# Residual rows in three steps, stores issued by ScalarE, modulated rows split out of PSUM, and four modulation vectors moved to the end of the first MLP

## The chip, the cores and the metric

One core of a Trainium2 chip runs the whole program. The metric is the device time of one execution in microseconds (us); less is better. PE is TensorE (matmuls, transposes), DVE is VectorE, ACT is ScalarE, POOL is GpSimd, and SP is SyncE, which here only issues DMA transfers. Each engine executes its own instruction stream strictly in order and meets the others at semaphores.

## The reference

Two layers of a diffusion trunk, 640 tokens (128 of a context, 512 latent ones) of width 1024, all fp32. Both layers modulate their input by six vectors that come from a condition, and end each sub-layer in a post-norm:

```python
def _adaln(cond, w, b):                       # w: 1024 x 6144, one per layer
    m = jax.nn.silu(cond) @ w + b
    return jnp.split(m[:, None, :], 6, axis=-1)

def _modulate(x, shift, scale):
    return x * (1 + scale) + shift

def _residual_norm(x, y, gate, g, b):
    return _layernorm(ALPHA * x + gate * y, g, b)

def _ffn(h, w1, w2):
    return jnp.square(jax.nn.relu(h @ w1)) @ w2
```

Layer 0 mixes by grouped-query attention and, beside it, a depthwise convolution of width 31; layer 1 by a bidirectional mLSTM whose gates run through scans over time. Each mixer has an output projection, `_residual_norm`, an MLP of width 4096 and again `_residual_norm`.

## The kernel before

The 640 tokens are five tiles of 128 rows; `acc` holds them in SBUF and `acc_d` in DRAM. Every large product is made to fp32 accuracy from three matmuls: an operand x is split into a high part (`whi`, `act_h`, cast on ACT) and a low part (`wlo`, `act_l`, a subtraction on POOL or DVE), and L193 to L195 multiply high by high, high by low and low by high. A weight piece is therefore a DMA into `raw` (L149), a cast (L166) and a subtraction (L167).

The program runs in stages, read from the trace: start, first modulation and the combined input projection until 180 us, with the convolution's taps (L965 on DVE, L972 on POOL) running beside it from 63 us on; twelve attention units until about 325 us, the convolution's LayerNorm (`conv_norm`, first matmul L1255) towards their end; the attention's output projection until 385; the first MLP until about 812, and behind it its tail: the last product `down(7)`, and for each tile the LayerNorm, four transposes per half (L375), the modulation and the first value projection of the mLSTM (`put_v`, head 0); then head 1 and the gates' product until 925; the mLSTM until 1214; its output projection until 1285; the second MLP until the end at 1735.

What sets the order: the program is written once in the order of the mathematics, and a list scheduler with a timeline model orders each engine's stream from it, with priorities. An instruction that waits for a buffer or for data stops all that stands behind it on its engine. For SP this holds too: a store whose data isn't there holds up the loads behind it.

Modulation vectors (1024 columns each) are made in background work. `ada_steps` yields after each of eight steps; a step loads 512 KB of `w_ada` and runs four matmuls of 32 output partitions side by side (L293); after the eighth comes one DVE addition (L297), and either a store (`gate_d`, for the two gate vectors of a layer) or two transposes (L305) and four copies. `background(n)` runs the next n steps of the `pending` list where it is called. Three vectors are made beside the input projection; seven, (0,5) and (1,0) to (1,5), during attention, because `ADA_IN_ATT = 7`; the attention's units call `background(7)` each. Vector (0,5) is the gate of the first MLP, and (1,0) and (1,1) modulate the rows that leave its tail; (1,2) to (1,5) are not needed before the mLSTM's output projection, at 1214 us.

The MLP keeps `acc_d` as the place of the residual: during the loop over its middle units, `residual(t, j)` loads half a row tile into `rx` (one buffer), multiplies and adds the LayerNorm's gain and bias on POOL (L445), and stores it. At the MLP's end `finish_mid` does per tile the LayerNorm and `modulate_T`:

```python
for half in range(2):
    pt = ...                                       # PSUM, four transposes into it
    h = scr(t, half)                               # SBUF
    affine(pt, half * 4, h, A, B, c, ...)          # L357 on DVE, L361 on ACT: h <- pt * A + B
    nc.scalar.copy(out=act_h, in_=h)               # L381
    nc.vector.tensor_tensor(out=act_l, in0=h, in1=act_h, op=subtract)   # L382
```

The output projection adds the gated product in 256-wide pieces (`add_gated`, L451 and L452): the first half of the columns through `s` and POOL, the second half in PSUM on DVE. `finish_mixer` stores `acc` to `acc_d` from SP; so does `put_v` its `v_d` pieces (L1397), and the tail its rows (L1431).

Of the kernel before, what the change touches and what calls it, by code (L numbers as in the profile page):

```python
# [18 lines left out]
P = 128  # L19
# [48 lines left out]
GEMMS = "01k2qr3"  # L68
ADA_IN_ATT = 7
FAST = (1, 3)  # L70
FIRST_DVE = ()
FIRST_HI = ((0, 0, 0), (0, 0, 1), (0, 1, 0), (0, 1, 1))
WIDE = False
AFF_DVE = (4,)
# [18 lines left out]
def trunk_kernel(ctx: ExitStack, tc: tile.TileContext, I, O):  # L93
# [231 lines left out]
    def drain():  # L325
        while pending:
            background()
# [37 lines left out]
    def modulate_T(src, t, A, B, scr, halves=(0, 1), second=nc.vector):  # L365

        ah, al = act
        c = 0 if t == 0 else 1
        sl = slice(t * P, (t + 1) * P)
        pt2 = None if K.startup else ps2()  # L370
        for half in halves:
            pt = psP.tile([P, 512], F32, name="po") if K.startup and t % 2 else ps1() if K.startup else pt2[:, half, :]
            for q in range(4):
                k = half * 4 + q
                nc.tensor.transpose(out=pt[:, q * P:(q + 1) * P], in_=src[:, k * P:(k + 1) * P], identity=ident)  # L375
            h = scr(t, half).rearrange("p (q n) -> p q n", n=P)
# [58 lines left out]

    def load_ln(lt, l, s, scale):
        nc.sync.dma_start(out=lt[:, 0, :], in_=I["ln_g"][l, s:s + 1, :].broadcast_to([P, D]))
        nc.sync.dma_start(out=lt[:, 1, :], in_=I["ln_b"][l, s:s + 1, :].broadcast_to([P, D]))
        if scale != 1.0:
            nc.scalar.mul(out=lt, in_=lt, mul=scale)  # L440
# [112 lines left out]
    class Sub:  # L553
# [51 lines left out]
        def rows(self, scale):  # L605
            self.gate, self.lnt = self.two_rows(), self.aux.tile([P, 2, D], F32, name="lnt")
            load_gate(self.gate, self.l, 0)
            load_ln(self.lnt, self.l, 0, scale)

# [5 lines left out]

        def residual(self, t, j):

            d = acc_d[:, t, j * 512:(j + 1) * 512]
            x = self.aux.tile([P, 512], F32, name="rx")
            nc.sync.dma_start(out=x, in_=d)  # L620
            residual_from(x, self.lnt, j, nc.gpsimd)
            nc.sync.dma_start(out=d, in_=x)

# [5 lines left out]
        def finish_mixer(self, key):  # L629
# [26 lines left out]
            def fin(t):  # L656
# [16 lines left out]
                if hi > HT:  # L673
                    b = max(lo, HT)
                    put("B12", self.h32[0][:, :, b:hi], slice(b - HT, hi - HT), PUT[2])
                    put("B22", self.h32[1][:, :, b:hi], slice(b - HT, hi - HT), PUT[3])
                nc.sync.dma_start(out=acc_d[:, t, :], in_=acc[:, t, :])
                if t and not COMB_LATE:
# [5 lines left out]

    def ffn(l, S, finish, ln_scale, prepare=None, ahead=None):
        w1, w2 = I["w_ff1"][l], I["w_ff2"][l]
# [105 lines left out]
        for j in range(6):  # L792
            for i in range(2):
                u = 2 * j + 2 + i
                h[u] = hidden(up(u))
                background(3)
                down(j, (h[2 * j], h[2 * j + 1]), i)
                if j < NT:
                    S.residual(j, i)
                background(2)  # L800
# [11 lines left out]
        S.lnt = late.tile([P, 2, D], F32, name="lnt")  # L812
        scr = late.tile([P, 4, 512], F32, name="scr")
        S.scratch = lambda t, half: scr[:, (t % 2) * 2 + half]
        rs0 = load_resid(0)
# [3 lines left out]
        pieces = [down_weights(7, c) for c in range(2)]  # L819
        load_ln(S.lnt, l, 1, ln_scale)  # L820
        rs1 = load_resid(1)
# [501 lines left out]
    def finish_mid(key, S):  # L1323
        def fin(t):
            layernorm(t, t == NT - 1)
            modulate_T(acc[:, t, :], t, *AB[key], S.scratch, second=nc.vector if t >= LATE_DVE else nc.scalar)
        return fin

    def finish_last(S):
        def moments(t):  # L1330

            x = acc[:, t, :]
            nm = smallp.tile([P, 1], F32, name="fl_m")
            if t in ACT_STATS:
                var = smallp.tile([P, 1], F32, name="fl_v")
                s, q = (smallp.tile([P, 2], F32, name=f"fl_{y}") for y in "sq")
                for j in range(2):
                    nc.scalar.activation(
                        out=S.scratch(t, j), in_=x[:, j * 512:(j + 1) * 512], func=AF.Copy, accum_out=s[:, j:j + 1])
                nc.vector.tensor_scalar(  # L1340
                    out=nm, in0=s[:, 0:1], scalar1=s[:, 1:2], scalar2=-1.0 / D, op0=ALU.add, op1=ALU.mult)
                for j in range(2):
                    nc.scalar.activation(
                        out=S.scratch(t, j), in_=x[:, j * 512:(j + 1) * 512], func=AF.Square, bias=nm[:, 0:1],
                        accum_out=q[:, j:j + 1])
# [47 lines left out]
    def put_v(ws, h, t, ps, tmp):  # L1393

        tm_tile(ws, act, t, ps[:, 0:256])
        nc.scalar.copy(out=tmp[:, 0:256], in_=ps[:, 0:256])
        nc.sync.dma_start(out=v_d[:, h, t], in_=tmp[:, 0:256])  # L1397

    with Sub(0) as S:
        S.rows(ALPHA)  # L1400
        out_proj(I["w_out_a"][0], S, S.finish_mixer("f0"))
        K.ada_m = lambda: S.fp.tile([P, 256], F32, name="ada_m")
        pending += [ada_vec(*x) for x in ada_late[ADA_IN_ATT:]]
        v_w = []

        def v_ahead():
            psum_plan(2, PS_D7)
            if PS_D7 < 3:
                K.psV = K.psum.enter_context(tc.tile_pool(name="psV", bufs=1, space=PSUM, reuse_waits="tile"))
            else:  # L1410
                K.psV = psC
# [11 lines left out]
        ffn(0, S, finish_and_v, ALPHA, lambda: mod_cols(1, 0, lng(0, 1), lnb(0, 1), *AB["m1"]), v_ahead)  # L1423
# [19 lines left out]
    with ExitStack() as ms:  # L1443
# [303 lines left out]
        def state(h, keys):  # L1747

            for d, (kwh, kwl) in enumerate(keys):
                cs = m2.tile([P, DEC], F32, name="wt").rearrange("p (a b) -> p a b", a=2)  # L1750
                for j in range(2):
# [5 lines left out]
                    nc.vector.tensor_copy(out=ncol[:, c0:c0 + 1], in_=ps[:, 256:257])  # L1757
                nc.sync.dma_start(
                    out=O["new_state_c"][0, 0, d, h].rearrange("(k p) v -> p k v", p=P), in_=cs)
# [122 lines left out]
    with Sub(1) as S:  # L1882
        S.rows(ALPHA)
        out_proj(I["w_out_m"][0], S, S.finish_mixer("f1"))
        ffn(1, S, finish_last(S), 1.0)

# [41 lines left out]
```

## Time and profile before

| what | before |
|---|---|
| median of 3 runs (lowest to highest) | 1737.89 us (1736.95 to 1741.92) |
| the profiled execution's own time | 1737.0 us |
| its span in the trace | 1735.2 us |
| mean granted TensorE clock | 0.971 of full speed |
| busy: PE, DVE, POOL, ACT | 1607.3, 1098.1, 1005.4, 796.3 us |
| PE idle in the span | about 128 us |

The time outside the span, 1.8 us, is the program's launch and end. [...] A row of groups gives busy time, mean duration of one instruction in ns, and behind the second bar the engine's idle time just before them with what ended it. Where an engine is shown as waiting for another, the wait is that of an in-order stream: what stands behind it waits as well.

### The profile page before, as it was taken

Reading aid. Unit: us, or ns where it says so; the run is one execution under the profiler, and the core shown is the slowest. Engines: PE = TensorE matmul, PEld = TensorE weight load, DVE = VectorE, ACT = ScalarE, POOL = GpSimd, SP = SyncE. Lnnn points to the kernel's source line nnn. Section 1 sums busy time; section 2 is a strip of 40 time slices with the busy share of each in tenths; the row PEclk is TensorE's granted clock in tenths of the full one; section 3 lists DMA queues with packets and bytes.
Section 4 is the critical chain, followed back from the end, with each engine's and each line's share of the span. In section 5 each row is a group of like instructions: output and inputs, shape, how many; then the busy total and the mean of one; then the engine's idle time right before and its main releaser. Section 6 shows DMA issues by size and latency. Waiting matters only on the chain. (4 is left out here: it accounts for less than half of the span.)

```text
span 1735.2 us, 27401 instructions
## 1 busy us (share of the span) xinstructions
PE 1607.3 (93%) x10155; PEld 1412.7 (81%) x10155; DVE 1098.1 (63%) x1924; ACT 796.3 (46%) x1560; POOL 1005.4 (58%) x760
## 2 busy tenths in 40 slices
PE   7988899998989999999788998997989999999996
PEld 4678555898879989987678998897979889989885
DVE  2899997669434444356875687778498354344367
ACT  2224666345444344343543555556265444344343
POOL 2246474247955546548654766756459756546565
PEclk8999999998999999999999999999999999999998
DMA  9852885323432213216223222235442323213241
GB/s 307 256 185 75 268 306 178 71 101 119 130 85 92 92 56 97 86 61 206 83 69 103 71 84 91 98 98 194 123 152 85 125 89 98 89 57 98 85 158 61
DMA packets 151309, 211.76 MB, mean 122 GB/s; under 512 B 11845, under 2 KB 92969, under 8 KB 151176
## 3 DMA queue, kind: packets, MB, share of 16 engines
q1 hardware_dynamic: 150944, 209.94, 37.4%
q8 instruction: 80, 1.31, 0.3%
q14 instruction: 53, 0.43, 0.1%
q10 hardware_dynamic: 232, 0.08, 0.0%
HBM read 186.74 MB, written 23.24 MB: 121 GB/s over the span
## 5 line engine op out<-in xcount | busy, mean ns | idle before, releaser
L167 POOL TENSOR_TENSOR wlo<-raw,whi 128x512 fp32r<-128x512 f32 x374 | 518.6, 1410 | 412.2 <-ACT whi L166 397.5
L166 ACT CAST whi<-raw 128x512 fp32r<-128x512 f32 x368 | 224.7, 620 | 429.2 <-PE ps L195 192.1
L193 PE MATMUL ps<-whi,h 128*128 128x512 f32 x640 | 254.5, 399 | 11.0 <-DVE pr L526 5.7
L194 PE MATMUL ps<-wlo,h 128*128 128x512 f32 x640 | 254.6, 398 | 0.3 <-POOL wlo L167 0.3
L195 PE MATMUL ps<-whi,h 128*128 128x512 f32 x640 | 253.6, 396 | 0.0
L193 PE MATMUL ps<-act_h,whi 128*128 128x320 f32 (+2 forms) x704 | 221.2, 316 | 8.5 <-ACT act_h L625 7.5
L194 PE MATMUL ps<-act_l,whi 128*128 128x320 f32 (+2 forms) x704 | 221.3, 315 | 5.5 <-DVE act_l L626 3.1
L195 PE MATMUL ps<-act_h,wlo 128*128 128x320 f32 (+2 forms) x704 | 220.9, 314 | 2.2 <-POOL wlo L167 2.2
L167 POOL TENSOR_TENSOR wlo<-s,whi 128x512 fp32r<-128x512 f32 x118 | 163.9, 1393 | 67.2 <-ACT whi L166 61.9
L758 DVE TENSOR_TENSOR acc<-acc,ps 128x512 f32<-128x512 f32 x120 | 81.8, 685 | 162.0 <-PE ps L195 162.0
L193 PEld LDWEIGHTS ps<-whi,h 128*128 128x128 f32 x640 | 121.3, 190 | 40.2 <-DVE pr L526 6.0
L193 PEld LDWEIGHTS ps<-act_h,whi 128*128 128x128 f32 x704 | 135.3, 192 | 13.2 <-ACT act_h L625 7.9
L195 PEld LDWEIGHTS ps<-whi,h 128*128 128x128 f32 x640 | 121.3, 190 | 29.2
L194 PEld LDWEIGHTS ps<-wlo,h 128*128 128x128 f32 x640 | 121.5, 190 | 28.1 <-POOL wlo L167 1.2
L194 PEld LDWEIGHTS ps<-act_l,whi 128*128 128x128 f32 x704 | 134.9, 192 | 8.9 <-DVE act_l L626 3.9
L195 PEld LDWEIGHTS ps<-act_h,wlo 128*128 128x128 f32 x704 | 134.9, 192 | 3.1 <-POOL wlo L167 3.1
L193 PE MATMUL ps<-whi,act_h 128*128 128x256 f32 x440 | 126.1, 290 | 0.3 <-DVE acc L1095 0.3
L194 PE MATMUL ps<-wlo,act_h 128*128 128x256 f32 x440 | 124.7, 287 | 0.0
L195 PE MATMUL ps<-whi,act_l 128*128 128x256 f32 x440 | 123.8, 287 | 0.0
L972 POOL TENSOR_TENSOR cy<-cy,tap 128x655 f32<-128x655 f32 x50 | 80.3, 1606 | 54.0 <-DVE cy L965 22.6
L193 PE MATMUL ps<-T_h,whi 128*128 128x320 f32 x336 | 103.7, 309 | 1.6 <-ACT pr L550 1.6
L166 ACT CAST whi<-s 128x512 fp32r<-128x512 f32 x120 | 73.2, 616 | 67.3 <-DVE s L501 54.9
(437 smaller groups left out, 4066.0 us busy)
## 6 DMA issues: line engine op xcount, KB each, us to landing
raw<-in_w_ff_dram SPq DMA_DIRECT2D x128, 512.0 KB
whi<-in_w_ada_dram SPq DMA_DIRECT2D x80, 256.0 KB
wlo<-in_w_ada_dram SPq DMA_DIRECT2D x80, 256.0 KB
raw<-in_w_in_m_dram SPq DMA_DIRECT2D x32, 512.0 KB
ada_w<-in_w_ada_dram SPq DMA_DIRECT2D x32, 256.0 KB
acc_d<-acc SPq DMA_DIRECT2D x15, 512.0 KB
raw<-in_w_in_a_dram SPq DMA_DIRECT2D x12, 512.0 KB
rx<-acc_d SPq DMA_DIRECT2D x20, 256.0 KB
```

Source lines behind the costliest of these rows:

```text
L166: nc.scalar.copy(out=hv, in_=src)
L167: (eng or nc.gpsimd).tensor_tensor(out=lv, in0=src, in1=f32(hv), op=ALU.subtract)
L193: nc.tensor.matmul(out=out, lhsT=lh, rhs=rh, start=start, stop=False)
L194: nc.tensor.matmul(out=out, lhsT=lh, rhs=rl, start=False, stop=False)
L195: nc.tensor.matmul(out=out, lhsT=ll, rhs=rh, start=False, stop=stop)
L758: nc.vector.tensor_tensor(out=x, in0=x, in1=ps, op=ALU.add)
L972: nc.gpsimd.tensor_tensor(out=y, in0=y, in1=tp, op=ALU.add)
```

## The change

- `ADA_IN_ATT` is 3: attention makes (0,5), (1,0) and (1,1), with the calls of `background` scaled to 3 a unit. The other four vectors enter `pending` in `v_ahead`, that is with the last product of the first MLP. Their 32 steps run at `background(5)` behind each of the five tiles of the tail, `background(1)` behind each value projection that follows, and a `drain`. Their weights go through `adaw`, 512 KB a step, three buffers.
- `WIDE` is on: the second half of an output projection goes through one 512-wide PSUM tile and one pair of 512-wide additions on DVE for each tile of rows.
- `modulate_T` of the tail writes the modulated rows back into PSUM; cast and subtraction read them there. The `scr` tile is gone but for the last LayerNorm.
- `residual(step)` has three parts that belong to three pieces: store of piece n-2, POOL work on piece n-1, load of piece n. `rx` has three buffers, the gain and bias tile half its size, loaded and scaled twice.
- Stores of `acc` in `finish_mixer`, of `v_d` and of `new_state_c` are issued by ACT.
- `put_v` uses its own one-buffer PSUM pool in the tail and the two-buffer pool `ps1` behind it, since `psc` now serves the vectors.

```diff
-ADA_IN_ATT = 7
+ADA_IN_ATT = 3
-WIDE = False
+WIDE = True
...
-            h = scr(t, half).rearrange("p (q n) -> p q n", n=P)
+            h = (scr(t, half) if K.startup else pt).rearrange("p (q n) -> p q n", n=P)
...
-        def residual(self, t, j):
-            d = acc_d[:, t, j * 512:(j + 1) * 512]
-            x = self.aux.tile([P, 512], F32, name="rx")
-            nc.sync.dma_start(out=x, in_=d)
-            residual_from(x, self.lnt, j, nc.gpsimd)
-            nc.sync.dma_start(out=d, in_=x)
+        def residual(self, step):
+            def rows(n):
+                return acc_d[:, n % NT, (n // NT) * 512:(n // NT + 1) * 512]
+            n = step - 2
+            if 0 <= n < 2 * NT:
+                nc.sync.dma_start(out=rows(n), in_=self.rx.pop(n))
+            n = step - 1
+            if 0 <= n < 2 * NT:
+                if n % NT == 0:
+                    nc.scalar.mul(out=self.lnt, in_=self.lnt, mul=self.scale)
+                residual_from(self.rx[n], self.lnt, 0, nc.gpsimd)
+            n = step
+            if n < 2 * NT:
+                if n % NT == 0:
+                    self.lnt = self.aux.tile([P, 2, 512], F32, name="lnt")
+                    load_ln(self.lnt, self.l, 0, (n // NT) * 512)
+                self.rx[n] = self.aux.tile([P, 512], F32, name="rx", bufs=3)
+                nc.sync.dma_start(out=self.rx[n], in_=rows(n))
...
-                nc.sync.dma_start(out=acc_d[:, t, :], in_=acc[:, t, :])
+                nc.scalar.dma_start(out=acc_d[:, t, :], in_=acc[:, t, :])
...
-                if j < NT:
-                    S.residual(j, i)
+                S.residual(2 * j + i)
...
-        nc.sync.dma_start(out=v_d[:, h, t], in_=tmp[:, 0:256])
+        nc.scalar.dma_start(out=v_d[:, h, t], in_=tmp[:, 0:256])
...
-        pending += [ada_vec(*x) for x in ada_late[ADA_IN_ATT:]]
...
+            K.psV = K.psum.enter_context(tc.tile_pool(name="psV", bufs=1, space=PSUM, reuse_waits="tile"))
             hv = [S.h_tile() for _ in range(2)]
+            K.ada_raw = lambda: S.late_pool.tile([P, D], F32, name="adaw", bufs=3)
+            pending.extend(ada_vec(*x) for x in ada_late[ADA_IN_ATT:])
...
-                put_v(v_w[0], 0, t, psC.tile([P, 512], F32, name="psc"), S.pr())
+                put_v(v_w[0], 0, t, K.psV.tile([P, 512], F32, name="psv"), S.pr())
+            background(5)
...
-            put_v(v_w[h], h, t, (psC if h == 0 else K.psV).tile([P, 512], F32, name="psc"), S.pr())
+            put_v(v_w[h], h, t, ps1(), S.pr())
+            background(1)
+        drain()
+        nc.scalar.mul(out=S.lnt, in_=S.lnt, mul=ALPHA)
```

PE's stream in the attention's early units, before (`kTA`, `kTB`: scores; `pT`: weights times values; `psc<-whi` and `psc<-wlo`: the two halves of an `ada` step):

```order
L1226 MATMUL po<-pT,vS 64x256 x2
L1200 MATMUL ps_2621<-ident,pp 128x128 x2
L293 MATMUL psc<-wlo,stat 32x256
L293 MATMUL psc<-whi,stat 32x256 x2
L293 MATMUL psc<-wlo,stat 32x256 x2
L1187 MATMUL ps_2753<-kTA,qT 128x320
L1187 MATMUL ps_2753<-kTB,qT 128x320
```

The same part of PE's stream with the change (its scores are L1197 there):

```order
L1236 MATMUL po<-pT,vS 64x256 x2
L1215 MATMUL ps_2509<-pT,vS 64x128 x2
L1150 MATMUL ps_2539<-identr,qs 128x128 x4
L1197 MATMUL ps_2596<-kTA,qT 128x320
L1197 MATMUL ps_2596<-kTB,qT 128x320
```

Up to this place both streams hold the same `ada` matmuls; from here on before has those of four vectors between the scores, and the change none.

PE's stream in the tail of the first MLP, with the change (`ps<-whi,h`: `down(7)`; `ident,acc`: transposes of a finished tile; `psv`: value projection):

```order
L195 MATMUL ps_8436<-whi,h 128x512
L193 MATMUL ps_8568<-whi,h 128x512
L194 MATMUL ps_8568<-wlo,h 128x512
L195 MATMUL ps_8568<-whi,h 128x512
L293 MATMUL psc<-adaw,stat 32x256
L375 MATMUL ps_8193<-ident,acc 128x128 x4
L293 MATMUL psc<-adaw,stat 32x256 x3
L375 MATMUL ps_8327<-ident,acc 128x128 x4
L193 MATMUL ps_8568<-whi,h 128x512
```

The 128 new matmuls stand in 22 places between `down(7)`, the transposes and the value projections; the last 20 of them, five steps, stand in one piece ahead of the 46 matmuls that precede the gates' product.

SP's stream between the value projections and the gates, before (`gwr`: the gates' weights; `nm_d<-g_ab`: the gates' result on its way to `mb`):

```order
L1397 DMA v_d<-pr 128x256
L1431 DMA acc_d<-acc 128x1024 x2
L1503 DMA gwr<-in_w_in_m_dram 128x8x16
L1513 DMA gb<-in_b_gate_m_dram 4x1 x3
L1397 DMA v_d<-pr 128x256 x2
L1513 DMA gb<-in_b_gate_m_dram 4x1
L1520 DMA m0c<-in_state_m_dram 4x1 x2
L1397 DMA v_d<-pr 128x256 x5
L149 DMA raw<-v_d 128x1024
L1397 DMA v_d<-wt 128x256
L149 DMA raw<-v_d 128x256
```

SP's stream from the last stores of finished rows to the gates, with the change:

```order
L1448 DMA acc_d<-acc 128x1024
L290 DMA adaw<-in_w_ada_dram 128x1024
L277 DMA ada_m<-in_b_ada_dram 4x256 x2
L290 DMA adaw<-in_w_ada_dram 128x1024 x4
L149 DMA raw<-v_d 128x1024
L290 DMA adaw<-in_w_ada_dram 128x1024
L149 DMA raw<-v_d 128x256
L300 DMA gate_d_1_8973<-ada_m 128x256
L149 DMA raw<-in_w_in_m_dram 128x4x256 x2
L1520 DMA gwr<-in_w_in_m_dram 128x8x16
L1530 DMA gb<-in_b_gate_m_dram 4x1 x4
```

The stores of `v_d` have left SP, and the load of the gates' weights, which stood ahead of most of them, now stands behind the last `adaw` load and behind the store of the last vector, `gate_d_1`.

## Rows read from the trace of the kernel before

**Rows 1.** The page's first part: busy time, share of span, instructions.
```profile
PE 1607.3 (93%) x10155; PEld 1412.7 (81%) x10155; DVE 1098.1 (63%) x1924; ACT 796.3 (46%) x1560; POOL 1005.4 (58%) x760
```

**Rows 2.** Windows in the attention; stretch, length, busy by engine, clock, DMA share, GB/s.
```profile
180.00:200.00 20.00, 14.52 (x124) 7.42 (x116) 18.08 (x35) 11.04 (x27) 9.00 (x7) 0.83 0.79 261
200.00:220.00 20.00, 17.42 (x146) 9.82 (x144) 19.02 (x40) 14.16 (x32) 11.54 (x10) 1.00 0.87 290
...
180.00:290.00 110.00, 99.85 (x817) 53.32 (x810) 96.31 (x194) 72.59 (x155) 65.77 (x46) 0.97 0.81 278
290.00:330.00 40.00, 39.31 (x273) 29.11 (x272) 33.48 (x75) 19.68 (x39) 2.54 (x2) 0.96 0.17 47
```

**Rows 3.** The same windows for line L293 alone, PE: the modulation vectors' matmuls.
```profile
180.00:290.00 110.00, 43.53 (x436) 0.97 0.81 278
...
180.00:183.00 3.00, 2.42 (x38) 1.00 0.86 264
```

**Rows 4.** Lines L972 and L1255: count, duration min/median/max, first and last start.
```profile
L972 POOL TENSOR_TENSOR cy<-cy,tap x50: 1339/1582/2670, 131.2 to 270.0; 128x655 f32<-128x655 f32 x50
...
L1255 PE MATMUL psc<-cy,ones x24: 274/326/433, 289.3 to 296.9; 128*128 128x128 f32 x8, 128*128 128x192 f32 x8, 128*128 128x320 f32 x8
```

**Rows 5.** Windows around the first MLP's tail and the value projections.
```profile
780.00:812.00 32.00, 29.33 (x153) 25.77 (x152) 21.20 (x25) 15.65 (x24) 27.37 (x20) 0.96 0.65 216
812.00:871.00 59.00, 49.21 (x266) 41.91 (x264) 45.44 (x99) 26.40 (x56) 37.61 (x28) 0.93 0.29 95
871.00:925.00 54.00, 42.82 (x311) 41.27 (x311) 35.70 (x44) 23.98 (x44) 30.39 (x21) 0.94 0.28 86
```

**Rows 6.** What PE waited for, 812 to 925: total us, times, longest.
```profile
PE psc L195 <- DVE act_l L382: 6.2, 3, 3.4
PE psc L193 <- ACT pr L1396: 4.5, 4, 1.7
PE psi L193 <- ACT wt L1396: 4.5, 1, 4.5
```

**Rows 7.** DVE groups, 812 to 875: busy us, mean ns, idle before.
```profile
L382 DVE TENSOR_TENSOR act_l<-scr,act_h 128x512 fp32r<-128x512 f32 x10 | 10.0, 1003 | 0.0
L451 DVE TENSOR_TENSOR ps<-ps,gate 128x512 f32<-128x512 f32 x6 | 4.1, 684 | 0.3 <-PE ps L195 0.3
L452 DVE TENSOR_TENSOR acc<-acc,ps 128x512 f32<-128x512 f32 x6 | 4.1, 677 | 0.1
```

**Rows 8.** DVE groups in the first output projection, 355 to 410.
```profile
L451 DVE TENSOR_TENSOR ps<-ps,h 128x256 f32<-128x256 f32 x10 | 4.3, 427 | 8.4 <-PE ps L195 8.4
L452 DVE TENSOR_TENSOR acc<-acc,ps 128x256 f32<-128x256 f32 x10 | 4.2, 415 | 0.2
```

**Rows 9.** Windows at the two MLPs' starts.
```profile
375.00:400.00 25.00, 23.79 (x196) 22.79 (x194) 24.48 (x46) 16.63 (x42) 17.56 (x13) 1.00 0.46 153
400.00:425.00 25.00, 18.53 (x88) 17.82 (x88) 24.79 (x22) 11.36 (x19) 16.95 (x8) 0.80 0.23 80
...
1275.00:1300.00 25.00, 18.12 (x140) 16.56 (x138) 24.77 (x45) 15.93 (x40) 16.89 (x13) 1.00 0.56 189
```

**Rows 10.** POOL's residual line L445; then waits of PE and POOL, 380 to 450.
```profile
L445 POOL TENSOR_TENSOR rx<-rx,lnt x40: 1261/1506/2544, 373.2 to 1377.2; 128x512 f32<-128x512 f32 x40
...
DMA rx<-acc_d: 60.7, 10
...
PE ps L193 <- ACT act_h L625: 5.8, 1, 5.8
PE ps L194 <- POOL act_l L626: 2.2, 1, 2.2
...
POOL rx L445 <- DMA rx<-acc_d: 7.7, 2, 7.0
```

**Rows 11.** What SP's queue waited for, 850 to 930.
```profile
SPq L1397 <- ACT pr L1396: 31.8, 6, 7.2
SPq L1431 <- DVE acc L445: 12.5, 4, 9.2
```

More of the change, by code (lines that the diff above doesn't have):

```diff
@@ L434, in layernorm, with load_ln @@
                 nc.scalar.activation(out=xs, in_=xs, func=AF.Identity, scale=r[:, 0:1], bias=b[:, 0:1])
[L436 to L440, printed above, removed]
+    def load_ln(lt, l, s, c0=0):
+        n = lt.shape[2]
+        for i, x in enumerate(("ln_g", "ln_b")):
+            nc.sync.dma_start(out=lt[:, i, :], in_=I[x][l, s:s + 1, c0:c0 + n].broadcast_to([P, n]))
     def residual_from(x, lt, j, eng):
@@ L605, in rows @@
         def rows(self, scale):
-            self.gate, self.lnt = self.two_rows(), self.aux.tile([P, 2, D], F32, name="lnt")
+            self.gate, self.scale, self.rx = self.two_rows(), scale, {}
             load_gate(self.gate, self.l, 0)
-            load_ln(self.lnt, self.l, 0, scale)
         def gate_room(self):
@@ L683, in finish_mixer, with ffn @@
             return fin
-    def ffn(l, S, finish, ln_scale, prepare=None, ahead=None):
+    def ffn(l, S, finish, prepare=None, ahead=None):
         w1, w2 = I["w_ff1"][l], I["w_ff2"][l]
@@ L812, in ffn @@
         S.lnt = late.tile([P, 2, D], F32, name="lnt")
-        scr = late.tile([P, 4, 512], F32, name="scr")
-        S.scratch = lambda t, half: scr[:, (t % 2) * 2 + half]
+        S.late_pool = late
         rs0 = load_resid(0)
@@ L819, in ffn @@
         pieces = [down_weights(7, c) for c in range(2)]
-        load_ln(S.lnt, l, 1, ln_scale)
+        load_ln(S.lnt, l, 1)
         rs1 = load_resid(1)
@@ L1325, in fin, with scratch @@
             layernorm(t, t == NT - 1)
-            modulate_T(acc[:, t, :], t, *AB[key], S.scratch, second=nc.vector if t >= LATE_DVE else nc.scalar)
+            modulate_T(acc[:, t, :], t, *AB[key], None, second=nc.vector if t >= LATE_DVE else nc.scalar)
         return fin
     def finish_last(S):
+        def scratch(t, half):
+            if not hasattr(S, "scr"):
+                S.scr = S.late_pool.tile([P, 4, 512], F32, name="scr")
+            return S.scr[:, (t % 2) * 2 + half]
         def moments(t):
@@ L1338, in moments @@
                     nc.scalar.activation(
-                        out=S.scratch(t, j), in_=x[:, j * 512:(j + 1) * 512], func=AF.Copy, accum_out=s[:, j:j + 1])
+                        out=scratch(t, j), in_=x[:, j * 512:(j + 1) * 512], func=AF.Copy, accum_out=s[:, j:j + 1])
                 nc.vector.tensor_scalar(
@@ L1343, in moments @@
                     nc.scalar.activation(
-                        out=S.scratch(t, j), in_=x[:, j * 512:(j + 1) * 512], func=AF.Square, bias=nm[:, 0:1],
+                        out=scratch(t, j), in_=x[:, j * 512:(j + 1) * 512], func=AF.Square, bias=nm[:, 0:1],
                         accum_out=q[:, j:j + 1])
@@ L1407, in v_ahead @@
             psum_plan(2, PS_D7)
[L1408 to L1411, printed above, removed]
+            K.psV = K.psum.enter_context(tc.tile_pool(name="psV", bufs=1, space=PSUM, reuse_waits="tile"))
             hv = [S.h_tile() for _ in range(2)]
+            K.ada_raw = lambda: S.late_pool.tile([P, D], F32, name="adaw", bufs=3)
+            pending.extend(ada_vec(*x) for x in ada_late[ADA_IN_ATT:])
             v_w.append(load_v(0, [
@@ L1420, in finish_and_v @@
             if t < NT - 1:
-                put_v(v_w[0], 0, t, psC.tile([P, 512], F32, name="psc"), S.pr())
-        ffn(0, S, finish_and_v, ALPHA, lambda: mod_cols(1, 0, lng(0, 1), lnb(0, 1), *AB["m1"]), v_ahead)
+                put_v(v_w[0], 0, t, K.psV.tile([P, 512], F32, name="psv"), S.pr())
+            background(5)
+        ffn(0, S, finish_and_v, lambda: mod_cols(1, 0, lng(0, 1), lnb(0, 1), *AB["m1"]), v_ahead)
         v_w.append(load_v(1))
         for h, t in [(1, t) for t in range(NT - 1)] + [(0, NT - 1), (1, NT - 1)]:
-            put_v(v_w[h], h, t, (psC if h == 0 else K.psV).tile([P, 512], F32, name="psc"), S.pr())
+            put_v(v_w[h], h, t, ps1(), S.pr())
+            background(1)
+        drain()
+        nc.scalar.mul(out=S.lnt, in_=S.lnt, mul=ALPHA)
         with tc.high_priority(offset=-RESID_BEHIND):
@@ L1757, in state @@
                     nc.vector.tensor_copy(out=ncol[:, c0:c0 + 1], in_=ps[:, 256:257])
-                nc.sync.dma_start(
+                nc.scalar.dma_start(
                     out=O["new_state_c"][0, 0, d, h].rearrange("(k p) v -> p k v", p=P), in_=cs)
@@ L1884, in trunk_kernel @@
         out_proj(I["w_out_m"][0], S, S.finish_mixer("f1"))
-        ffn(1, S, finish_last(S), 1.0)
+        ffn(1, S, finish_last(S))
 _INS = ["x_prompt", "x_sample", "cache_k", "cache_v", "state_c", "state_n", "state_m", "c", "c_ctx",
```

## The prediction

> **What bounds the kernel now.** I read the busy times first, then windows by stage, then the waits in the stages that the change touches. PE is busy 1607.3 us of 1735.2 [rows 1], so nearly all of the time is PE's work, and an edit can gain only in two ways: by taking work off PE where PE is full and others are not, or by putting work into PE's holes, 128 us in all. The change tries both with the same work: four of the ten vectors leave the attention and enter the first MLP's tail. So two stages decide it.
>
> In the attention PE and DVE are both nearly full: of the 110 us from 180 on PE is busy 99.85 and DVE 96.31 [rows 2]. The reader is to see that DVE comes close behind PE, so that what PE loses is not simply gained. In the tail, 812 to 925, PE is busy 92.03 of 113 us, at a clock of 0.93 and 0.94 [rows 5]: 21 us of holes, and the three largest causes of them, 15.2 us together, are waits of a value projection for ACT or DVE [rows 6], in which PE could run other matmuls. At the start of each MLP the bound is DVE, at 24.48 to 24.79 us of 25 [rows 9].
>
> **The vectors out of the attention.** L293 takes 43.53 us of PE for 436 records [rows 3]. One vector has 8 steps of 4 matmuls with two records each, 64 records, so four vectors are 256, and 43.53 x 256 / 436 = 25.6 us of PE leave. What remains on PE in the 110 us is 74.3; DVE keeps its 96.3 but for four additions. DVE is then what ends last. It would need 96.3 us if it never waited. It filled 19.02 of 20 us in its best stretch, 95%, and 18.08 of 20, 90%, in the first [rows 2], where PE was already the less busy of the two. At 95% the stretch takes 101.4, a gain of 8.6; at 90% 107, a gain of 3; at 100% a gain of 13.7. I take 9, since the 95% was reached with PE not full either. The convolution allows it: its last POOL operation begins at 270.0 and its LayerNorm at 289.3 [rows 4], so 17 us of shift are free there. From 290 to 330, with PE at 39.31 of 40 [rows 2], no vector's matmul stands, and I expect nothing. Attention: -9, from -14 to 0.
>
> **The vectors into the tail.** The same 256 records come back. Their price is 25.6 us as the attention paid it, in short pieces and partly at a low clock; the densest piece of the trace ran 38 records in 2.42 us [rows 3], which makes 16.3 us. I take 21, halfway, because the new order holds both short and long pieces. Of that, the 15.2 us of waits in rows 6 can be filled, for the steps stand between the value projections and transposes that wait there. 21 - 15 = +6. The ends: everything filled and the cheap price, 16.3 - 21 = -5; nothing filled at the dear price, +26.
>
> The loads move too, and they queue on SP. 32 loads of 512 KB are 16.8 MB. The DMA engines moved 278 GB/s at a share of 0.81 [rows 2], 343 GB/s at full share, so the loads need 48.9 us of all engines. Other traffic from 812 to about 890 takes 0.29 x 59 + 0.28 x 19 = 22.4 us [rows 5]. Together 71 of 78 us, a share of 0.91; the busiest 20 us in rows 2 have 0.87. It just fits, with three buffers and no reserve. At the attention's mean of 0.81 it would take 88 us, 10 more than there are; this lies inside the ends above and gets a rival.
>
> **The rows split out of PSUM.** Ten subtractions of L382 take 1003 ns each from SBUF; operations of the same 512 columns with one operand in PSUM take 684 and 677 [rows 7]. 10 x 0.32 = 3.2 us less on DVE, which is busy 45.44 of 59 us there [rows 5]; and 6.2 us of PE's waits are for just this line [rows 6], which the vectors' matmuls are to fill already. I count -1, from -3 to +1. [...]
>
> **The wide additions.** Before, a tile pays 2 x (427 + 415) = 1684 ns [rows 8]; the wide pair 684 + 677 = 1361 [rows 7]. That is 0.32 x 5 = 1.6 us less on DVE for each output projection. DVE is full only from 375 on [rows 9], where two or three of the tiles fall, so about 0.75 each, -1.5 for both. The adverse end is a later first addition, since one tile now waits for both weight pieces: +1. Range -3 to +1.
>
> **Residual in three steps.** POOL waited 60.7 us for `rx`, in ten waits [rows 10]; that goes. In the loop PE never waits for it. It can matter at an MLP's start only, where PE waited 2.2 us for POOL's `act_l`; the 5.8 us before it are ACT's `act_h` [rows 10]. In the first MLP 16 residual operations now stand ahead of that `act_l` on POOL, 11 before: 5 x 1.5 = 7.5 us more work against 7.7 us less waiting. I count 0. Ends: -2 for each MLP (the wait goes), and +4 for each: DVE's subtractions with both operands in SBUF take 0.3 us more when POOL works beside them [rows 7], some dozen of them stand at each start, 12 x 0.3 = 4, and DVE is what is full.
>
> **Stores on ACT.** SP stood 31.8 us behind `v_d` stores and 12.5 behind the tail's `acc` stores [rows 11] (the latter stay on SP); the loads behind them were late. No wait of PE in rows 6 is for a DMA, so I count -1, from -3 to +1, the loss being ACT's issue time ahead of casts. [...]
>
> **Sum.** -9 + 6 - 1 - 1.5 + 0 - 1 = -6.5 against the profiled execution's own 1737.0: 1730.5. The median lies 0.9 above that execution, so I forecast 1731.
>
> **The rivals.**
> First, the tail hides all and the attention reaches DVE's limit: -13 there, -1 in the tail, -3 for the rest, 1721. For it: 21 us of holes and a clock of 0.93 that fewer holes would raise. Against it: DVE never ran at 100% over 20 us.
>
> Second, slower: the tail becomes a queue of loads. SP executes in order; an `adaw` load waits until PE has used the buffer three steps earlier, and behind it stand the weights of the value projections and of the gates. The load of the gates' weights was ahead of most `v_d` stores; it now comes after the last vector's store, and the gates' scans follow it. If PE finds nothing else, the full price of 25.6 us is paid and no hole filled: -9 + 25.6 - 3 = +13, 1750. It decides from the point where the tail's DMA share must pass the 0.87 that the trace shows. It speaks against it that 46 matmuls stand between the last step and the gates' product.
>
> Third, the attention gives nothing. With 74.3 of 110 us PE would be as little busy as from 180 to 200 (14.52 of 20), where the granted clock was 0.83 [rows 2]. [...]
>
> Fourth, the three-step residual does more harm than good at both MLP starts: +8 in place of 0, 1739.
>
> **How the numbers follow.** About 0.3%, 5.2 us, is what a measurement of this kernel can tell from no change: faster is below 1732.7, slower above 1743.1. The forecast's case has 0.40, of which 0.26 lies below 1732.7 and 0.14 above; the first rival 0.20, all faster; the second 0.19, all slower; the third 0.13, of which 0.04 slower; the fourth 0.08, of which 0.04 slower. Faster 0.46, same 0.27, slower 0.27. The range leaves out the lower half of the first rival and the upper half of the second: 1719 to 1748. The forecast's own range is 1726 to 1738.
>
> **What would show it.** In the profile after: the first matmuls of the output projection come about 9 us earlier than 325, with DVE at 95% or more from 200 to 290; if DVE stays at 90% and the clock falls under 0.9 there, the third rival is right. The stretch from `down(7)` to the gates' product grows by about 6 us, PE's waits for L382 and for the evictions shrink to a third, and the clock is near 1; if PE waits for `adaw` or DMA share exceeds 0.87, the second. L382 takes about 0.69 us. POOL's waits for `rx` are gone, and DVE at the MLPs' starts is full as before. The prediction is wrong if the vectors cost PE more than 26 us in their new place, or if a stage that the change does not touch moves by more than 3 us.

## The result and the profile after

The changed kernel takes 1764.76 us (median of 4 runs, 1760.66 to 1765.87) against 1739.64 us of the kernel before (median of 4 runs): a ratio of 1.014, 95% interval 1.0122 to 1.0158. It is 25 us slower, where 1731 us was forecast.

The page after, first part, answers to [rows 1]:

```profile
PE 1615.6 (92%) x10155; PEld 1415.2 (80%) x10155; DVE 1090.6 (62%) x1904; ACT 796.1 (45%) x1562; POOL 1000.7 (57%) x760
```

PE has the same 10155 matmuls and is busy 8 us longer; DVE is busy 7.5 us less. The span grew by 23.7 us, so two thirds of the loss are idle time of PE and not work. Where it came from is seen when the same instructions of both traces are laid side by side:

| the same instruction in both traces | before, us | after | shift |
|---|---|---|---|
| first 320-column score of the attention | 185.3 | 186.6 | +1.3 |
| last addition of the convolution | 270.0 | 286.4 | +16.4 |
| last product of the attention | 324.3 | 319.3 | -5.0 |
| first cast of the convolution's rows (`act_h<-cy`) | 325.8 | 329.2 | +3.4 |
| first addition of the first MLP's down product | 507.7 | 506.7 | -1.0 |
| last copy of a value projection | 940.6 | 961.3 | +20.7 |
| transposes at the mLSTM's end (`ncol`) | 1214.3 | 1230.9 | +16.6 |
| sixth addition of the second MLP's down product | 1418.8 | 1443.1 | +24.3 |
| last addition of it | 1694.6 | 1719.5 | +24.9 |

The output projection reads two halves, the attention's rows and the convolution's; the cast `act_h<-cy` makes the second ready. So there are three places: the attention with the convolution beside it, which was to give 9 us and lost 2; the first MLP's tail, which was to cost 6 and cost about 18 by the mLSTM's end (22 by the last value copy); and the second MLP's start, which was to cost nothing and cost about 8. One place gained: the first MLP's start, 4.4 us; why is not shown.

Windows after, columns as in [rows 2] and [rows 5] (the stretch and its length; the busy time of PE, its weight loads, DVE, ACT and POOL with their instructions in brackets; the granted clock of TensorE as a share of full speed; the mean busy share of the 16 DMA engines; GB/s): the attention, one stretch of it, and the tail with what follows.

```profile
180.00:290.00 110.00, 89.22 (x608) 55.05 (x606) 98.59 (x190) 76.76 (x165) 67.42 (x45) 0.83 0.39 130
...
260.00:280.00 20.00, 13.12 (x65) 8.98 (x61) 18.86 (x32) 15.89 (x33) 13.46 (x9) 0.64 0.22 79
...
812.00:871.00 59.00, 57.32 (x410) 40.51 (x409) 42.77 (x99) 23.57 (x48) 31.78 (x26) 1.00 0.70 239
871.00:905.00 34.00, 26.51 (x244) 19.09 (x243) 7.27 (x26) 9.48 (x20) 9.49 (x10) 0.88 0.77 270
905.00:960.00 55.00, 44.23 (x301) 43.11 (x301) 37.34 (x39) 22.25 (x42) 25.27 (x18) 0.89 0.23 70
```

In the attention the DMA share fell from 0.81 to 0.39, as the loads left, and the clock from 0.97 to 0.83. PE is busy only 10.6 us less: the vectors' matmuls take 24 us less (19.45 in place of 43.53), the others more, since more of them fall into the stretch and some run at the low clock. In the tail PE is full until 871 (57.32 of 59, clock 1.00): the vectors' matmuls did fill the holes. Then follow 34 us in which DVE, ACT and POOL do little (7.27, 9.48 and 9.49 us), PE is busy 26.51 us at a clock of 0.88, and the DMA share is 0.77. What PE and SP's queue waited for there, 812 to 960 and 805 to 925 (first PE, then SP; total, times, longest):

```profile
PE psi L193 <- ACT wt L1411: 9.0, 3, 4.8
PE psc L293 <- DMA adaw<-in_w_ada_dram: 8.9, 9, 2.1
...
SPq L290 <- PE psc L293: 31.3, 22, 5.2
SPq L290 <- DMA adaw<-in_w_ada_dram: 12.9, 8, 3.0
...
SPq L300 <- DVE m0c L1524: 6.8, 1, 6.8
```

PE waits nine times for an `adaw` tile, and SP stands 31.3 us before its next `adaw` load because PE has not yet used the tile three steps earlier. Each waits for the other in a ring of three. The waits for DVE and ACT of [rows 6] are gone but for `wt`, now 9.0 us in a longer window.

The convolution and its rows' first cast, by line (duration min/median/max, first and last start), answer to [rows 4]:

```profile
L982 POOL TENSOR_TENSOR cy<-cy,tap x50: 1338/1578/2667, 132.5 to 286.4; 128x655 f32<-128x655 f32 x50
...
L1265 PE MATMUL psc<-cy,ones x24: 274/326/432, 290.4 to 297.8; 128*128 128x128 f32 x8, 128*128 128x192 f32 x8, 128*128 128x320 f32 x8
...
L1304 ACT CAST act_h<-cy x8: 297/456/619, 329.2 to 333.7; 128x128 fp32r<-128x128 f32 x4, 128x512 fp32r<-128x512 f32 x4
```

The last tap now starts at 286.4, 16.4 us later than before, and the convolution's LayerNorm 4 us behind it, where it was 19. The 17 us of slack that the prediction counted on are used up by the convolution itself. On PE the output projection comes to the end of the attention's half and waits for the convolution's (180 to 330; before has no such wait):

```profile
PE ps L193 <- ACT act_h L1304: 2.4, 1, 2.4
```

### The profile page after: what moved, and what is told of

The parts are those of the page before. It is cut to its first block, busy times and chain, and to the rows that moved or that the text cites. A ratio compares the mean times of both kernels' runs of the same rounds, so it can differ in the third digit from the quotient of the medians.

```text
span 1758.9 us, 27294 instructions
## 1 busy us (share of the span) xinstructions
PE 1615.6 (92%) x10155; PEld 1415.2 (80%) x10155; DVE 1090.6 (62%) x1904; ACT 796.1 (45%) x1562; POOL 1000.7 (57%) x760
## 4 chain that ended last, share of the span: by engine, by line
PE 55%; DVE 20%; DMA 11%; POOL 6%; issue 4%; ACT 3%; SPq 1%; DVEq 0%; POOLq 0%; ACTq 0%
PE ps L193 16%; PE ps L194 16%; PE ps L195 15%; DVE cy L975 4%; DMA raw<-in_w_in_m_dram 3%; POOL wlo L167 3%; DMA raw<-in_w_ff_dram 2%; DMA ada_w<-in_w_ada_dram 2%; POOL rx L445 2%; PE psc L293 2%; DMA adaw<-in_w_ada_dram 1%; PE ps L1229 1%; PE po L1236 1%; DVE act_l L638 1%; PE ps L1197 1%
## 5 line engine op out<-in xcount | busy, mean ns | idle before, releaser
L193 PE MATMUL ps<-whi,act_h 128*128 128x256 f32 x480 | 139.3, 293 | 2.8 <-ACT act_h L1304 2.4
L194 PE MATMUL ps<-wlo,act_h 128*128 128x256 f32 x480 | 137.6, 289 | 0.0
L195 PE MATMUL ps<-whi,act_l 128*128 128x256 f32 x480 | 136.3, 290 | 1.2 <-DVE act_l L1305 1.2
L195 PE MATMUL ps<-T_h,wlo 128*128 128x320 f32 x336 | 105.1, 313 | 5.9 <-POOL wlo L167 5.9
```

The costliest lines, as they stand in the source:

```text
L193: nc.tensor.matmul(out=out, lhsT=lh, rhs=rh, start=start, stop=False)
L194: nc.tensor.matmul(out=out, lhsT=lh, rhs=rl, start=False, stop=False)
L195: nc.tensor.matmul(out=out, lhsT=ll, rhs=rh, start=False, stop=stop)
```

## The experiments

### All vectors back in the attention

```diff
-ADA_IN_ATT = 3
+ADA_IN_ATT = 7
```

> The changed kernel with all seven vectors back in the attention (ADA_IN_ATT 7); every other part of the change stays. Theory A, the moved vectors alone cost the time: they made the output projection of the attention start 3.4 us later and the mLSTM end 16.6 us later, so this kernel should lie at 1735 to 1745 us, level with the kernel before. Theory B, the other parts (stores on ScalarE, PSUM split, residual in three steps, wide additions) reordered the streams for the worse: it stays above 1752.

1745.63 us, ratio 1.0041 (1.0025 to 1.0057). Neither theory in full, though A's range ends at 1745: the moved vectors cost 1.0140 - 1.0041, about 17 us, the other parts together about 7. In its trace the value projections end 1.6 us later than before and the first MLP's tail has no net loss; its loss is at the second MLP's start, 7.6 us.

### The tail without the steps, with one load, with half loads

```diff
-        for k in range(KT):
+        for k in range(0 if K.bias_only else KT):
...
-        nc.vector.tensor_tensor(out=m, in0=ps[:, 0:256], in1=m, op=ALU.add)
+        if not K.bias_only:
+            nc.vector.tensor_tensor(out=m, in0=ps[:, 0:256], in1=m, op=ALU.add)
```

> The changed kernel without the 32 steps in the tail: vectors (1,2) to (1,5) are taken from their bias alone, so their loads and matmuls are left out. Theory A, the steps lengthen the tail and nothing hides them: the gates and the mLSTM come 15 to 20 us earlier than in the changed kernel, the time is 1742 to 1750, and the attention's output projection still starts at about 329. Theory B, the reordered streams of the tail cost the time and not the steps: above 1757.

```diff
+            K.one = K.ada_raw()
+            nc.sync.dma_start(out=K.one, in_=wk(I["w_ada"][1])[:, 0, 2 * D:3 * D])
...
+            if K.one is not None:
+                raw = raw[:, 0:512], raw[:, 512:1024]
```

> The changed kernel with all 128 matmuls of the tail's steps, but on one loaded weight tile: 31 of the 32 loads of 512 KB are left out. Theory A1, the loads (DMA share 0.70 to 0.77, three buffers, SP's order) make the tail late: 1745 to 1752. Theory A2, TensorE's own work does, since the holes were too few: 1757 to 1763, less the 9 us that TensorE was seen waiting for these loads at most.

```diff
+            K.ada_raw = lambda: S.late_pool.tile([P, 512], F32, name="adaw", bufs=3)
+            K.one = S.late_pool.tile([P, 512], F32, name="one")
...
+                nc.sync.dma_start(out=raw, in_=wv[:, k, runs[0][0]:runs[0][0] + 512])
+                raw = raw, K.one
```

> The changed kernel with half of every tail load: each step loads 256 KB instead of 512, and takes the other half from a tile loaded once; 8.4 MB are left out, the 32 loads, three buffers and all matmuls stay. With all loads the value projections end 20.7 us later than before, with one load 0.9. Theory bytes (the ring of three buffers waits for the transfer itself): the delay falls by about half or more, to 3 to 11 us, time 1746 to 1755. Theory queue (SP waits in order, whatever the size): it stays above 16, time above 1759.

| kernel | ratio (95% interval) | last value copy, us | shift of the `ncol` transposes since the down product's last addition |
|---|---|---|---|
| change, 32 loads of 512 KB | 1.0140 (1.0122 to 1.0158) | 961.3 | +17.7 |
| 32 loads of 256 KB | 1.0057 (1.0034 to 1.0079) | 951.5 | +12.7 |
| one load, all matmuls | 1.0021 (1.0005 to 1.0038) | 941.5 | +1.1 |
| no loads, no matmuls | 1.0081 (1.0060 to 1.0102) | 949.9 | +2.2 |

The 128 matmuls cost next to nothing: with one load the tail is as long as without the steps. That the kernel without steps is nevertheless the slower of the last two has another place: it came into the tail 8.5 us late already, from the first output projection and MLP start, where its streams had come out in another order. The loads cost 16.6 of the 17.7 us. By total the kernel with one load, 1743.18 us, came out below the range of its theory A1, and the one without steps, 1751.70, just above that of A. Windows of the kernel with one load, the same stretches as after:

```profile
812.00:871.00 59.00, 59.00 (x429) 44.21 (x428) 42.94 (x109) 24.95 (x50) 32.54 (x28) 1.00 0.31 103
871.00:905.00 34.00, 33.67 (x287) 29.83 (x286) 21.43 (x28) 12.26 (x28) 18.64 (x13) 1.00 0.24 73
905.00:960.00 55.00, 47.38 (x339) 46.02 (x338) 40.58 (x49) 28.56 (x51) 37.50 (x27) 0.94 0.33 96
```

Where PE was busy 26.51 of 34 us at a clock of 0.88, it is now full at 1.00. Over the three stretches it is idle 8.0 us, with all loads 19.9. With half the bytes the whole run regains 0.83 of the 1.19 points between all loads and one, the last value copy 9.8 of its 19.8 us, and PE's waits for `adaw` shrink from 8.9 to 0.4 us (one wait): the theory of bytes, at 1750.12 us. SP's wait for PE is no measure of the harm, for it is longer here, 38.4 us. So the size of the transfers matters and not only their number or SP's order. But by the mLSTM's end the tail has regained only 5 of 16.6 us, and since each kernel's streams are ordered anew, the split between bytes and queue is not settled. The number of buffers was not varied.

The gates are a second part of it. Their weights' load stands behind the last vector's store on SP, and ACT waited for it (waits of ACT after, 905 to 960):

```profile
ACT gw_h L1533 <- DMA gwr<-in_w_in_m_dram: 8.0, 1, 8.0
```

The gates' scans begin 30.1 us later than before (936.1 against 906.0), the last value copy comes 20.7 later, so less of the value projections is left to run beside the scans. With one load the scans begin 6.5 us later than before, with half loads 27.4, which fits what the half loads did not regain. This share was not measured by itself.

### Fewer taps, and taps at a higher priority

```diff
-                    for k in range(1, CONV_K):
+                    for k in range(1, CONV_K - 8 * (i == 3)):
```

> The changed kernel without the last 8 of 31 taps on the fourth channel block of the convolution: work left out, one multiplication on ScalarE and one addition on GpSimd for most of them. Theory C, the convolution's serial chain (last addition at 286.4 us, 270.0 before) sets where the output projection starts: it starts 7 to 14 us earlier than 329 and the time falls to 1751 to 1758. Rival: the attention's own chain on VectorE sets it; the time falls by 0 to 4 us only.

```diff
-CONV_BEHIND = 1500
+CONV_BEHIND = -1500
```

> The changed kernel with the convolution's taps at a higher priority for the scheduler, nothing left out. Theory C (the convolution's serial chain starts the LayerNorm of the convolution and with it the output projection late): the last addition comes earlier than 286, and the output projection starts earlier than 329 by about as much, up to 8 us. Rival: the taps displace the attention's own operations on VectorE and ScalarE, the last product of the attention moves from 319 towards 325, and nothing is won: the start stays at 327 to 331.

Times in us since the first 320-column score of each trace's attention:

| kernel | last tap | LayerNorm of the convolution | first cast of the convolution's rows |
|---|---|---|---|
| before | 84.7 | 104.0 | 140.5 |
| change | 99.8 | 103.8 | 142.6 |
| change, taps at a higher priority | 91.7 | 96.8 | 137.9 |
| change, 8 taps fewer | 82.9 | 88.4 | 132.1 |

With the change the cast follows the convolution's last tap by 43 to 49 us in all three kernels; before, with PE full, it followed by 56. Eight taps fewer bring it 10.5 us forward, to 8.4 us ahead of the kernel before, nearly the 9 us that I had forecast. So the convolution's serial chain is what the attention's gain ran into. A second sign of it: with the change the cast comes 9.9 us behind the attention's last product (319.3 to 329.2), before and with eight taps fewer 1.5 us (317.0 to 318.5 in the latter). The higher priority shows less. The cast came at 327.6 in place of 329.2, and the last product moved back to 323.5, as its rival expected. The line that shows it, eight taps fewer:

```profile
L1304 ACT CAST act_h<-cy x8: 299/459/622, 318.5 to 323.7; 128x128 fp32r<-128x128 f32 x4, 128x512 fp32r<-128x512 f32 x4
```

Neither is faster as a whole: 1768.72 us (1.0182, 1.0154 to 1.0211) with fewer taps, which cannot be told from the change, and 1789.7 us (1.0269) with the higher priority. They lost it behind the attention, in a place the change does not touch: DVE waits in the output projections for the gate rows, at the second one 15.5 us with fewer taps and 15.0 with the higher priority, which pays at the first one too. (With fewer taps another 7 us went within the mLSTM; their cause is open.) From the trace with higher priority, 325 to 365:

```profile
DVE s L451 <- DMA h<-gate_d: 13.4, 2, 8.3
```

The load of `gate_d` stands on SP behind a weight load that waits for its buffer (5 waits on `wlo`, the longest 13.4 us, at the second output projection). In the changed kernel the same load happens to stand ahead of it there, and DVE does not wait for it; at the first output projection it waits 3.1 us.

### Three vectors in the attention, nothing else

```diff
-ADA_IN_ATT = 7
+ADA_IN_ATT = 3
```

> The kernel before with only the number of vectors in the attention changed from seven to three: the other four run in the middle of the first MLP, where TensorE is full (25.0 us of 25). Theory: the output projection starts 1 to 4 us later than before, as with the whole change, and the first MLP grows by 16 to 26 us, TensorE's price of 256 records, while the tail stays as it was: 1755 to 1768. Rival, my prediction's reading: the attention gains 9 us and the sum is 1746 to 1756.

1770.5 us, ratio 1.0164 (1.0149 to 1.0179). The convolution's rows are cast 2.9 us later than before, and from there to the last addition of the first down product the kernel grows by 17.9 us, both as the theory said. The total lies above its 1768, since 14.5 us more come at the mLSTM's output projection, where this order, too, has DVE wait 14.3 us for the gate's rows:

```profile
DVE s L451 <- DMA h<-gate_d: 14.3, 2, 7.3
```

It confirms with every other part of the change absent that taking four vectors out of the attention gains nothing.

### The other parts, one by one

The kernel before with `residual(step)`, the half-size gain tile and three `rx` buffers of the change:

> The kernel before with the residual in three steps alone. In every kernel with the whole change the second MLP starts late: from the mLSTM's last transpose to the sixth addition of the down product it takes 7.6 us longer (with all vectors back in the attention). Theory D, the three-step residual does it (GpSimd's bunched residual work in front of weight splits, and the gate's load behind the last residual step): 1743 to 1749 here. Theory E, wide additions or the stores do: 1735 to 1741.

The kernel before with wide additions:

```diff
-WIDE = False
+WIDE = True
```

> The kernel before with the 512-wide second half of the output projections alone. My prediction gave this part -1.5 us. Theory: 1737 to 1741, within what can be told. Rival E: the wider PSUM tile moves the order at the start of the MLPs and costs 3 to 8 us: 1743 to 1749.

The kernel before with the stores moved:

```diff
-                nc.sync.dma_start(out=acc_d[:, t, :], in_=acc[:, t, :])
+                nc.scalar.dma_start(out=acc_d[:, t, :], in_=acc[:, t, :])
...
-        nc.sync.dma_start(out=v_d[:, h, t], in_=tmp[:, 0:256])
+        nc.scalar.dma_start(out=v_d[:, h, t], in_=tmp[:, 0:256])
```

> The kernel before with the 38 stores (acc in the mixers' ends, v_d, new_state_c) issued by ScalarE alone. My prediction gave this part -1 us. Theory: 1736 to 1741. Rival: moving stores changes where SP issues gate and weight loads and costs 3 us or more: above 1743.

The change with seven vectors in the attention and the old residual:

```diff
-                S.residual(2 * j + i)
+                if j < NT:
+                    S.residual(j, i)
```

> The changed kernel with all vectors in the attention and the residual of the kernel before: what is left of the change are wide additions, the split from PSUM, the stores on ScalarE and the value projections' PSUM buffers. With the three-step residual the same kernel took 0.41% more than before, 5 to 8 us of it at the second MLP's start. Theory D, the residual costs them: the second MLP's start returns to within 3 us of before and the time is 1735 to 1741. Theory E: it stays at 1744 or more.

The same without wide additions:

> The kernel before with only the stores on ScalarE, the split from PSUM and the two-buffer value projections: the three parts in which the runs showed no loss. Stores alone stood 2 us earlier behind the first MLP's tail. If their gains add, 1733 to 1738, faster than before by up to 0.4%; if the new order of the start of an MLP eats it, 1738 to 1744.

| kernel | median, us | ratio (95% interval) |
|---|---|---|
| before + three-step residual | 1741.81 | 1.0013 (0.9991 to 1.0035) |
| before + wide additions | 1741.71 | 1.0003 (0.9983 to 1.0022) |
| before + stores on ACT | 1738.03 | 0.9986 (0.9967 to 1.0005) |
| change, seven vectors in the attention | 1745.63 | 1.0041 (1.0025 to 1.0057) |
| the same, old residual | 1745.64 | 1.0015 (1.0002 to 1.0029) |
| the same, old residual, narrow additions | 1744.00 | 1.0013 (1.0002 to 1.0025) |

None of the three parts tried alone can be told from no change; the split from PSUM and the value projections' new PSUM pools were not tried alone. Taking the three-step residual out of the set with seven vectors gives 0.26 points back, some 4.5 us, but the two intervals overlap (the medians stand on different chips; the ratios are what compares). By its total that kernel meets theory E, by the second MLP's start theory D. The last kernel of the table gained nothing further.

The traces do not settle the place either. From the mLSTM's end (`ncol`) to the sixth addition of the second MLP's down product they lose against before:

| kernel | residual | loss, us |
|---|---|---|
| change | three steps | 7.7 |
| change, seven vectors | three steps | 7.6 |
| before + three-step residual | three steps | 5.5 |
| change, seven vectors, old residual | old | 2.2 |
| the same, narrow additions | old | 5.7 |

The last row has the old residual and loses as much as the third, whose traced execution, 1746.38 us, was moreover 4.6 above its median. What the three-step residual does show is a full POOL (the fifth number). The stretch 1325 to 1350 in the second MLP's start, first the change, then the change with seven vectors; the stretches hold different matmuls, so PE's numbers are not to be compared:

```profile
1325.00:1350.00 25.00, 21.04 (x119) 20.19 (x119) 16.74 (x15) 12.56 (x20) 25.00 (x14) 0.93 0.37 122
```

```profile
1325.00:1350.00 25.00, 21.01 (x102) 18.10 (x103) 13.00 (x16) 11.54 (x19) 25.00 (x18) 0.93 0.42 137
```

The same stretch with the old residual:

```profile
1325.00:1350.00 25.00, 20.10 (x91) 17.83 (x90) 18.11 (x19) 13.90 (x25) 22.34 (x15) 0.80 0.36 116
```

With the three-step residual POOL is busy 25.00 of 25, and PE waits there for `wlo` from POOL, in the change:

```profile
PE ps L195 <- POOL wlo L167: 4.0, 3, 2.8
```

In the kernel before with that residual alone it is 5.8 us. With the old residual PE has no wait for `wlo` in the stretch; it waits for DVE and ACT instead, 4.9 us in all. So PE's wait for a POOL that is busy with residual work is seen in three kernels, while its price in the time, between nothing and 5 us, is not settled, and what costs the second MLP's start its 8 us stays open.

The version with the best measured ratio, stores alone, cannot be told from the kernel before, and none was measured faster than it.

## Why the prediction was wrong

**What bounds the kernel.** Right as read: PE and DVE together in the attention, holes in the tail, DVE at the MLPs' starts.

**The vectors out of the attention: wrong, -9 forecast, about +2 measured.** PE lost the vectors' matmuls, and the units ran ahead: the scores were up to 13 us earlier, the last product 5.0. The step that failed is the sentence "The convolution allows it": it took the last tap's time, 270.0, as given. The taps have a low priority with the scheduler and share ACT, POOL and DVE with the units. When the units come sooner, the taps go later; DVE's order now has the last of its taps behind 16 of its 32 copies of attention weights, before behind 13. The chain from the last tap to the cast of the convolution's rows is longer than what is left of the attention, so it decides. The signs that the prediction set for the third rival came true: from 200 to 290 the clock was 0.85 and DVE at 89%. The eight taps show that this was not what ended last, for with that many fewer the rows came 10.5 us earlier, with DVE no fuller and the clock at 0.89. But of the 9 us the units gave 6.3 (the last product came 5.0 earlier though the first score came 1.3 later), and that the low clock took the rest is not excluded.

**The vectors into the tail: PE's term too dear, the loads' missing.** The matmuls cost +1 instead of +6: all holes filled, as in the first rival. The loads were the failure. "It just fits" compared 71 us of transfers with 78 us of time, found a share of 0.91 against 0.87 seen, and charged nothing. The 0.87 was not the highest of the kernel before, which held 1.02 from 240 to 260:

```profile
240.00:260.00 20.00, 18.98 (x173) 10.33 (x165) 18.78 (x38) 13.73 (x30) 12.55 (x10) 1.00 1.02 377
```

So the DMA engines had reached more than the tail got out of them: there the share was 0.70 and 0.77, where SP and PE wait for each other around three buffers. By the sum's own other line, 88 us at a share of 0.81, the term would have been +10; at the measured 0.73 over the two stretches it is, as an estimate after the fact, 71 / 0.73 = 97, +19, and +17.7 came, part of it by way of the gates. The second rival had the mechanism and the place. Its size was luck: its 25.6 us were the price of matmuls with no hole filled, and the matmuls cost 1; nor did the share pass 0.87, its condition. Its chance of 0.19 was too low for a load sum that left no reserve.

**Split from PSUM.** Right in size. The group after, 812 to 905, and the same line before, with the shortest, median and longest duration:

```profile
L382 DVE TENSOR_TENSOR act_l<-ps,act_h 128x512 fp32r<-128x512 f32 x10 | 6.9, 685 | 5.5 <-ACT act_h L381 5.5
...
L382 DVE TENSOR_TENSOR act_l<-scr,act_h x10: 674/682/1774, 836.6 to 872.4; 128x512 fp32r<-128x512 f32 x10
```

685 ns where 0.69 us was forecast, 3.1 us less than [rows 7]; whether the time gained by it was not measured alone. The prediction read the mean of 1003 ns as the price of each. In fact four of the ten took 1174 to 1774 ns, each with POOL at work throughout, and six took 674 to 683, two of them with POOL at work. After the change none takes more than 692, POOL at work or not. So what left is the delay that these four had beside POOL; which of POOL's operations cause it is open.

**Wide additions.** The durations came as forecast (694 and 680 ns against 684 and 677), the time did not move: 1.0003 (0.9983 to 1.0022), which does not exclude the -1.5 of the sum.

**Residual in three steps.** The fourth rival's place, at the second MLP alone, but not its mechanism: it charged DVE's subtractions, and the runs show PE waiting for POOL's `wlo`. That this makes the 8 us of the place is not shown. That POOL's waits for `rx` are gone was wrong; what ended them, after:

```profile
DMA rx<-acc_d: 50.2, 5
```

Five waits in place of ten, nearly the same sum: the first loads wait for the mixer's own store of `acc` (SP stood 28.1 us for it at the first MLP). The 0 that I set for POOL's order held at the first MLP, where the start even gained 4.4 us (PE's wait of 5.7 us for DVE at 502 is not there after), and missed at the second, by 8 us whose cause is open.

**Stores on ACT.** -1 forecast, 0.9986 measured, an interval that holds 0 and the -1 alike. Each of the 30 stores of `acc` and `v_d` that ACT issues after the change occupied it for 0.3 to 0.4 us. The 31.8 us behind `v_d` of [rows 11] are gone; with the stores moved alone, SP waits elsewhere, 850 to 930:

```profile
SPq L149 <- POOL wlo L167: 30.9, 4, 23.6
SPq L1431 <- DVE acc L445: 23.1, 5, 12.1
```

So the queue, relieved of one wait, stood in the next; by the total, nothing behind it was urgent.

## What to carry to other kernels

When work is taken off the bounding engine, ask of each low-priority chain beside it whether it keeps its time or is pushed back by what now comes sooner; its end, not the sum of the next engine's busy time, can be the new bound. When background work is moved into holes, do not price its loads by the full rate: with a ring of three buffers the DMA share was 0.70 to 0.77 here, where the attention had reached 1.02. And look up which small, urgent load then stands behind them on the same queue. A change to one part reordered streams far from it in these scheduled kernels: 7 to 15 us came and went with the place of one gate load on SP, so an experiment has to be read stage by stage before its total is believed.

## What was not expected of the hardware

The granted clock was 0.5 of full speed from 265.6 to 282.7 us after, 17 us on end, while PE was far from idle: it was busy 13.12 of 20 us from 260 on, and its longest single wait there was 3.1 us. Before, the same stretch of work, with the vectors' matmuls between, ran at 1.00. The traces side by side bear it out: from 180 to 290 the clock is 0.95 to 0.97 in all seven kernels that make seven vectors in the attention, and 0.83 to 0.88 in all seven that make three, also in the pairs that differ in nothing else (0.97 against 0.83 with the change, 0.97 against 0.86 without); over the whole span of the profiled executions it is 0.965 to 0.971 against 0.956 to 0.963. So the clock stood higher with the background matmuls in the attention, and that paid a part of their price. From the first score (181.7 before, 183.0 after) to the last product, PE's busy time for the attention's other matmuls is 96.6 us before and 101.2 after, so this part is an estimated 5 of the 25 us.
